# Renumbering the rows of q and k in a hybrid attention block on one Trainium2 core

## The chip, the cores and the metric

The kernel runs on one core of a Trainium2 chip. The metric is device microseconds (us) of one execution; the figure for the kernel before is the median of three. A core has five instruction streams that run side by side and wait for each other through semaphores: PE (TensorE matrix products), DVE (VectorE), ACT (ScalarE), POOL (GpSimd) and SP (SyncE). Here SP does no arithmetic: it issues all DMA transfers of the program, one after the other. PE works on tiles of 128 partitions and writes to PSUM; all other tiles lie in SBUF, which has 128 partitions as well.

## The reference, cut to what matters

One decoder block on 1024 tokens of 1024 features, in float32. Its token-mixing half projects the normed input into the heads of two mixers and attends in both:

```python
h = rms_norm(x, g_attn_pre[l]) * (1 + sc_a) + sh_a
proj = h @ w_in[l]
qa = partial_rope(proj[..., :o1].reshape(b, s, A_Q_HEADS, HEAD_DIM), cos, sin)
ka = partial_rope(proj[..., o1:o2].reshape(b, s, A_KV_HEADS, HEAD_DIM), cos, sin)
...
qb = partial_rope(proj[..., o3:o4].reshape(b, s, B_HEADS, HEAD_DIM), cos, sin)
kb = partial_rope(proj[..., o4:o5].reshape(b, s, B_HEADS, HEAD_DIM), cos, sin)
...
oa = banded_attention(qa.reshape(b, s, A_KV_HEADS, A_GROUP, HEAD_DIM), ka, va,
                      A_WINDOW - 1, sink=sink_a[l])
ob = dilated_mixture_attention(qb, kb, vb).reshape(b, s, B_W).astype(x.dtype)
mixed = jnp.concatenate([rms_norm(oa, g_mix_a[l]), rms_norm(ob, g_mix_b[l])], axis=-1)
x = x + gt_a * rms_norm(mixed @ w_out[l], g_attn_post[l])
h = rms_norm(x, g_mlp_pre[l]) * (1 + sc_m) + sh_m
x = x + gt_m * rms_norm(jnp.square(jax.nn.relu(h @ w_up[l])) @ w_down[l], g_mlp_post[l])
```

Mixer A has 8 query heads and 2 key heads of 64 features, mixer B has 8 of each. The rotation (`partial_rope`) touches the first 16 features of a head. A score is a sum over a head's 64 features, so the order in which these features are summed is free as long as q and k have the same one.

## The kernel before, in words

Each float32 operand of a product is split into a high part that is exact in PE's fast float32r format and the low rest. The projections take three products for one (high times high, low times high, high times low); the scores take a q whose 128 contraction rows hold each feature twice.

The work has stages. Up to about 60 us, x is loaded, normed and transposed, the modulation vectors are computed, and the first projection runs. From there to about 410 us six units are projected (units 0 and 1 are the two key heads of A with their four query heads each, units 2 to 5 are two heads of B each) in two halves x of 512 tokens and three column blocks c of 128, and the attention of the units that are ready runs between these products. Then come the output projection, and from about 570 us a squared-ReLU MLP.

A column block of the projection leaves PSUM in `evac` (L734). Block c = 0 holds the rotated features and is rotated on DVE (L757 to L760); the others are copied. In both cases the result becomes a pair of high and low part in a 4 KB-per-partition staging tile `hl`: ACT writes the high part (L763, L774), DVE or POOL the low one (L766, L777). There are five staging tiles in all (`r_stg`, L385), and they are shared with the loads of the modulation weights (`wa_st`, L994) and the gates (`gate_st`, L1034 and L1035).

From `hl` the features go by DMA to the tiles that the scores read, `qt` (128 rows x 4 x 512) and `kt` (128 rows x 2 x 1024). This is called a set-down here; it is `f_st` (L792), issued on SP at L803. Row 64 i + r of `qt` and of `kt` holds feature row r, in copy i. In a B unit both copies of q are the same, with high and low part side by side in a row, and copy 0 of k is its high part, copy 1 its low part; in an A unit q and k change places in this. So each feature is sent twice, by two DMAs. In an A unit one partition of `qt` takes the four heads of a feature from four partitions of `hl`.

Which feature stands on which partition of `hl` is set by `PARTS_A` and `PARTS_B` (L66 to L68): tuples (first partition, count, step, q or k, first row of qt or kt) for each column block. `ROWS_A` and `ROWS_B` (L70, L71) give the head feature of each row. The columns of w_in are put into that order on the host (`_columns`), and `tables` (L700) lays the cosines and sines on the partitions that hold rotated features: POOL fills `rows` (L707, L713), PE transposes it (L719), ACT copies it out (L721).

What sets the order is a planner (`Sched`, L175). Every operation is given to it with an estimated duration, what it depends on and which buffers it takes and gives back; it keeps a clock for each engine and emits the instructions in the order that these clocks give. Each engine then runs its own list strictly in that order. A DMA is planned with 0.62 us of SP for each issue and its bytes over 345 GB/s; a set-down of n issues enters as one step. A unit's scores may be planned once all set-downs of that half are planned to have landed (`st.posted`, `need`).

At most eight DMAs are under way: SP hands its DMAs to eight semaphores in turn, and an issue waits until the DMA before it on the same semaphore has landed.

Of the kernel before, what the change touches and what calls it, by code (L numbers as in the profile page):

```python
# [10 lines left out]
F32 = mybir.dt.float32  # L11
# [22 lines left out]
def _split_const(value, top, bits, count):  # L34
    parts, rest, unit = [], value, 2.0 ** (top - bits)
    for _ in range(count):
# [26 lines left out]

PARTS_B = (((0, 64, 2, "q", 0), (1, 64, 2, "k", 0)), ((0, 64, 2, "q", 32), (1, 64, 2, "k", 32)), ())  # L66
PARTS_A = (((0, 32, 2, "q", 0), (64, 32, 2, "q", 32), (1, 64, 2, "k", 0)),
           ((0, 96, 1, "q", 8), (96, 32, 1, "q", 40)), ((0, 64, 1, "q", 48),))  # L68

ROWS_B = [*range(0, 8), *range(16, 24), *range(8, 16), *range(24, 64)]  # L70
ROWS_A = [*range(0, 8), *range(16, 40), *range(8, 16), *range(40, 64)]  # L71


def _columns():

    out = []
    for u in range(6):
        if u > 1:
            q = [512 + 128 * u + 64 * h for h in range(2)]
            k, v = [x + 512 for x in q], [x + 1024 for x in q]  # L80
            parts, rows = PARTS_B, ROWS_B
        else:
            g = u
            q, k, v = [256 * g + 64 * h for h in range(4)], [512 + 64 * g], [640 + 64 * g]
            parts, rows = PARTS_A, ROWS_A
        for c in range(3):
            got = [h + d for h in v for d in range(64)] if c == 2 else []
            got = [0] * (P - len(got)) + got
            for p, n, step, whose, row in parts[c]:
                heads = q if whose == "q" else k  # L90
                got[p:p + n * step:step] = [h + rows[row + r] for r in range(n // len(heads)) for h in heads]
            out += got
    return out

# [254 lines left out]
def hybrid_block(ctx: ExitStack, tc: tile.TileContext, x, positions, w_ada, b_ada, g_attn_post, w_in, w_out,  # L349
# [34 lines left out]
    r_pj, r_x, r_t, r_s, r_o, r_d = Res(2), Res(1), Res(2), Res(2), Res(1), Res(0)  # L384
# [96 lines left out]
    r_wa, r_acc = Res(NWA), Res(2)  # L481
# [20 lines left out]
    def place0(name):  # L502
        return p0.tile([P, 1024], F32, name=name, tag="wa", bufs=NWA)
# [196 lines left out]
    def tables(groups, place, r_place, r_bank, bank, deps):  # L700

        for i in range(2):
# [20 lines left out]
                                   gives=[(r_bank, 1)], prio=2))  # L723

    e_tab = [[], []]
    tables([(0, 2, 4), (1, 2, 1)], lambda: place0("rows"), r_wa, r_t,
           lambda: pt.tile([P, 4, P], F32, name="ptab", tag="t"), [[], []])


# [4 lines left out]
    def evac(u, x, c, get_ps, done, r_bank):  # L734

        isb = u > 1
        parts = (PARTS_B if isb else PARTS_A)[c]
        cs = slice(512 * x, 512 * x + 512)
        b = {}
        e_q.setdefault((u, x), [])  # L740
        e_k.setdefault((u, x), [])

        def posted():
            n_in[u, x] = n_in.get((u, x), 0) + 1
            if n_in[u, x] == 3:
                st.posted += 1

        def f_new():
            b["f"] = stage("hl")[:].rearrange("p (s t) -> p s t", s=2)
            b["t"] = b["f"].bitcast(F32R)  # L750

        if c == 0:
            def f_rope():
                f_new()
                ps, t = get_ps(), b["f"][:, 1]
                cos, sin = tabs[0][:, cs], tabs[1]
                V.tensor_tensor(t[64:128], ps[0:64], sin[0:64, cs], ALU.mult)  # L757
                V.tensor_tensor(t[0:64], ps[64:128], sin[64:128, cs], ALU.mult)
                V.tensor_tensor(ps[:], ps[:], cos, ALU.mult)
                V.tensor_tensor(t, t, ps[:], ALU.add)  # L760
            e0 = e_rot[u, x] = op("DVE", 4 * t_dv(512), f_rope, [done] + e_tab[x], takes=[(r_stg, 1)],
                                  gives=[(r_bank, 1)], prio=2)
            eh = op("ACT", t_sb(512), lambda: A.copy(b["t"][:, 0], b["f"][:, 1]), [e0], prio=2)  # L763

            def f_lo(eng):
                return lambda: eng.tensor_tensor(b["t"][:, 1], b["f"][:, 1], b["f"][:, 0], ALU.subtract)  # L766
            el = op(("DVE", "POOL"), (t_dv(512), t_ptt(512)), (f_lo(V), f_lo(G)), [eh], prio=2)
        elif parts:
            n = P if c < 2 else parts[-1][1]
            sc_ = scl[0] if isb else None  # L770

            def f_hi():
                f_new()
                A.mul(b["t"][:n, 0], get_ps()[:n], -0.125 if sc_ is None else sc_[:n])  # L774

            def f_lo():
                V.scalar_tensor_tensor(b["t"][:n, 1], get_ps()[:n], -0.125 if sc_ is None else sc_[:n],  # L777
                                       b["f"][:n, 0], ALU.mult, ALU.subtract)
            eh = op("ACT", t_ps(512) + AP_COST, f_hi, [done, e_rot[u, x]], takes=[(r_stg, 1)], prio=2)
            el = op("DVE", t_dv(512) + AP_DV, f_lo, [eh], gives=[(r_bank, 1)] if c < 2 else [], prio=2)  # L780

        if parts:
            for whose in ("k", "q") if c == 0 else ("q", "k"):
                mine = [a for a in parts if a[3] == whose]
                if not mine:
                    continue
                both = isb == (whose == "q")
                nh = 2 if isb else 4 if whose == "q" else 1
                for s_ in ((0, 1) if not both else (None,)):
                    new = c == 0 and whose == "k" and s_ in (0, None)  # L790

                    def f_st(s_=s_, new=new, mine=mine, whose=whose, nh=nh, both=both):  # L792
                        if new:
                            if not x:
                                ks[u] = kring.tile([P, 2, 1024], F32R, name="kt", tag="kt")
                            qs[u, x] = qring.tile([P, 4, 512], F32R, name="qt", tag="qt")
                        dst = qs[u, x][:] if whose == "q" else ks[u][:, :, cs]
                        for p0_, n_, step, _, row in mine:
                            src = b["f"][p0_:p0_ + (n_ - 1) * step + 1:step]
                            m_ = n_ // nh  # L800
                            for i in range(2) if both else (s_,):
                                o = dst[64 * i + row:64 * i + row + m_].bitcast(F32)
                                nc.sync.dma_start(o, src if both else src[:, s_])  # L803
                    if new:
                        e_new[u, x] = Ev()
                    last = (whose == ("q" if c == 0 or not isb else "k")) and s_ in (1, None)

                    def after(new=new, last=last):
                        if new:
                            e_new[u, x].t = 0.0  # L810
                        if last and c < 2:
                            posted()
                    by = sum(a[1] * 2048 * (4 if both else 1) for a in mine)
                    e = load(f_st, by, [eh if s_ == 0 else el] + ([] if new else [e_new[u, x]]),
                             takes=[(r_k, 1 - x), (r_q, 1)] if new else [], prio=-12, n=len(mine) * (2 if both else 1),
                             gives=[(r_stg, 1)] if last else [], after=after)
                    (e_q if whose == "q" else e_k)[u, x].append(e)
        if c < 2:
            return
        nh = 2 if isb else 1  # L820
        o = P - 64 * nh

        def f_vt():
            b["vt"] = prp.tile([P, 512], F32, name="vt", tag="vt", bufs=1)
            A.copy(b["vt"][:64 * nh], get_ps()[o:])
        e = op("ACT", t_ps(512), f_vt, [done] + ([el] if parts else []), takes=[(r_vt, 1)], gives=[(r_bank, 1)], prio=2)

        def f_pv():
            b["pv"] = px.tile([P, 4, 64 * nh], F32, name="pv", tag="x")
            for j in range(4):  # L830
                T.transpose(b["pv"][:, j], b["vt"][:64 * nh, j * P:(j + 1) * P], ident[:64 * nh, :64 * nh])
        e = pe_op("post", 0.43, f_pv, [e], takes=[(r_x, 1), (r_v, 1)], gives=[(r_vt, 1)])

        def part(s_):
            return vs[u, x][:, :, :nh, s_], b["pv"][:].rearrange("p j (h d) -> p j h d", h=nh)

        def f_vh():
            vs[u, x] = vring.tile([P, 4, 2, 2, 64], F32R, name="v_hl", tag="v")
            A.copy(*part(0))

        def f_vl():
            V.tensor_tensor(part(1)[0], part(1)[1], part(0)[0].bitcast(F32), ALU.subtract)
        e = op("ACT", t_ps(256 * nh), f_vh, [e], prio=2)
        op("DVE", t_dv(256 * nh), f_vl, [e], gives=[(r_x, 1)], prio=2, after=posted)
# [1230 lines left out]
```

## Time and profile before

| | |
|---|---|
| median of three runs | 1163.08 us (1161.61 to 1167.61) |
| the profiled execution | 1161.99 us |
| its span, first to last instruction | 1160.2 us |
| PE busy | 1117.1 us, 96% of the span |
| DVE, ACT, POOL busy | 815.4, 639.2 and 261.1 us |
| mean granted TensorE clock | 0.986 |
| DMA | 185.31 MB, 51.1% of 16 engines' span on SP's queue |

Busy time is summed over instructions, so that 96% leaves some 43 us in which PE ran nothing. The profile's views give for any stretch of time how long each engine was busy, the granted clock of TensorE, the share of the 16 DMA engines' time that was in use and the rate in GB/s. The view of waits names, for an instruction that had to wait, what ended the wait; a wait for several semaphores is put down to one of them only, so the tile's name is to be read with care. The chain of waits follows the work that ended last back to what released it.

### The profile page before, as it was taken

To read this page: it belongs to the slowest core of one execution; us is meant where nothing else is said; L and a number is where in the kernel's file an instruction comes from. 1 tells how busy PE (TensorE), PEld (TensorE's weight loads), DVE (VectorE), ACT (ScalarE), POOL (GpSimd) and SP (SyncE) were. 2 spreads that over 40 slices of the span, in tenths; PEclk is the share of its full clock that TensorE was granted. 3 is DMA by queue.
4 is the path that set the end of the run, shared out by engine and by line. 5 is a ranking of instruction groups with operands and counts; after the bars stand their busy time and mean duration, and the time that the engine had idled before them with its cause. 6 is when DMAs were issued, how large, how long until landed. Compare 5 with 4: busy or idle time off the path is not lost.

```text
span 1160.2 us, 15646 instructions
## 1 busy us (share of the span) xinstructions
PE 1117.1 (96%) x5416; PEld 926.6 (80%) x5416; DVE 815.4 (70%) x1380; ACT 639.2 (55%) x1105; POOL 261.1 (23%) x344
## 2 busy tenths in 40 slices
PE   8989989999999899998999999999999999999996
PEld 7768778788888787887788888888888888888885
DVE  7848576566666775658969665499653796547998
ACT  7949676455555774667676524563233732246542
POOL 2347667566663441112000000000000000000002
PEclk9989989999999989999999999999999999999998
DMA  9477857465545614554683057812369212585103
GB/s 351 161 174 168 168 120 182 111 153 122 134 102 130 156 48 139 193 181 182 257 314 118 19 207 274 315 50 89 120 220 326 106 55 73 184 306 181 37 19 146
DMA packets 90944, 185.31 MB, mean 160 GB/s; under 512 B 8432, under 2 KB 31088, under 8 KB 90864
## 3 DMA queue, kind: packets, MB, share of 16 engines
q1 hardware_dynamic: 90864, 184.30, 51.1%
q8 instruction: 43, 0.70, 0.3%
q14 instruction: 37, 0.30, 0.1%
HBM read 137.08 MB, written 28.31 MB: 143 GB/s over the span
## 4 chain that ended last, share of the span: by engine, by line
PE 70%; DVE 10%; DMA 7%; issue 4%; POOL 4%; ACT 3%; SPq 2%; DVEq 0%; POOLq 0%; ACTq 0%
PE mlp_ps L1898 16%; PE mlp_ps L1899 16%; PE mlp_ps L1897 16%; PE pj L861 3%; PE pj L864 3%; PE pj L862 3%; PE s_ps L1122 2%; PE o_ps L1257 1%; DMA wa<-in_w_ada 1%; SPq L803 1%; PE pt_ps L1227 1%; DMA wa_st<-in_w_ada 1%; DVE hw L1668 1%; PE pt_ps L1230 1%; PE s_ps L1177 1%
## 5 line engine op out<-in xcount | busy, mean ns | idle before, releaser
L1897 PE MATMUL mlp_ps<-hw 128*128 128x512 f32 x896 | 349.7, 390 | 1.2 <-ACT hw L1659 1.2
L1898 PE MATMUL mlp_ps<-hw 128*128 128x512 f32 x896 | 348.7, 389 | 1.1 <-DVE hw L1665 1.1
L1899 PE MATMUL mlp_ps<-hw 128*128 128x512 f32 x896 | 348.6, 389 | 0.0
L1897 PEld LDWEIGHTS mlp_ps<-hw 128*128 128x128 f32 x896 | 168.2, 188 | 36.8 <-ACT hw L1659 1.6
L1898 PEld LDWEIGHTS mlp_ps<-hw 128*128 128x128 f32 x896 | 168.2, 188 | 36.8 <-DVE hw L1665 1.4
L1899 PEld LDWEIGHTS mlp_ps<-hw 128*128 128x128 f32 x896 | 168.2, 188 | 34.9
L1668 DVE TENSOR_TENSOR hw<-w,hw 128x1024 fp32r<-128x1024 f32 x96 | 114.5, 1219 | 94.7 <-ACT hw L1661 94.4
L1661 ACT CAST hw<-w 128x1024 fp32r<-128x1024 f32 x96 | 97.5, 1047 | 129.8 <-PE mlp_ps L1899 97.5
L1997 POOL TENSOR_TENSOR st<-st,nhalf 128x1 f32<-128x1 f32 x8 | 7.8, 978 | 601.9 <-DVE st L1995 601.9
L861 PE MATMUL pj<-hw,w_hl 128*128 128x512 f32 x240 | 104.2, 434 | 0.0
L864 PE MATMUL pj<-hw,w_hl 128*128 128x512 f32 x240 | 95.5, 398 | 0.0
L862 PE MATMUL pj<-hw,w_hl 128*128 128x512 f32 x240 | 95.3, 397 | 0.0
L1245 DVE TENSOR_TENSOR ph<-pt_ps,ph 128x512 fp32r<-128x512 f32 (+1 forms) x110 | 69.7, 648 | 36.0 <-ACT ph L1241 35.7
L1661 ACT CAST hw<-u 128x1024 fp32r<-128x1024 f32 x48 | 48.7, 1052 | 64.6 <-PE mlp_ps L1899 64.6
L1241 ACT CAST ph<-pt_ps 128x512 fp32r<-128x512 f32 (+1 forms) x110 | 59.5, 555 | 32.1 <-PE pt_ps L1230 27.0
L1668 DVE TENSOR_TENSOR hw<-u,hw 128x1024 fp32r<-128x1024 f32 x48 | 57.0, 1218 | 18.2 <-ACT hw L1661 18.2
L1148 ACT ACTIVATE p_sb<-p_sb,mn 128x128 f32<-128x128 f32 (+3 forms) x64 | 49.7, 777 | 36.3 <-DVE mn L1141 34.9
L1955 DVE TENSOR_TENSOR yacc<-yacc,mlp_ps 128x512 f32<-128x512 f32 x96 | 62.1, 681 | 3.3 <-PE mlp_ps L1899 3.3
L1153 POOL TENSOR_SCALAR p_sb<-p_sb,den 128x128 f32<-128x128 f32 (+3 forms) x64 | 49.0, 775 | 47.8 <-DVE den L1151 44.6
L1010 POOL TENSOR_TENSOR ada_acc<-ada_acc,wa_st 128x512 f32<-128x512 f32 x42 | 55.5, 1320 | 3.5
L864 PEld LDWEIGHTS pj<-hw,w_hl 128*128 128x128 f32 x240 | 45.6, 190 | 10.7
L1473 PE MATMUL y_ps<-hw,oh 128*128 128x512 f32 x128 | 51.7, 404 | 0.0
(205 smaller groups left out, 2010.6 us busy)
## 6 DMA issues: line engine op xcount, KB each, us to landing
hw<-s_dram SPq DMA_DIRECT2D x84, 512.0 KB
wa_st<-in_w_ada SPq DMA_DIRECT2D x32, 512.0 KB
w<-in_w_up SPq DMA_DIRECT2D x32, 512.0 KB
w<-in_w_down SPq DMA_DIRECT2D x32, 512.0 KB
s_dram<-hw SPq DMA_DIRECT2D x28, 512.0 KB
w_st<-in_w_in SPq DMA_DIRECT2D x36, 256.0 KB
x_sb<-in_x SPq DMA_DIRECT2D x16, 512.0 KB
wa<-in_w_ada SPq DMA_DIRECT2D x32, 256.0 KB
```

The source lines that it names most:

```text
L861: T.matmul(ps, w[:, 0, n], h[0], start=(k == 0), stop=False)
L862: T.matmul(ps, w[:, 1, n], h[0], start=False, stop=False)
L864: T.matmul(ps, w[:, 0, n], h[1], start=False, stop=(k == KC - 1))
L1010: G.tensor_tensor(ada.acc[:, :512], ada.acc[:, :512], wa[:, j], ALU.add)
L1241: A.copy(b["ph"][:, 0, :w], b["pt"][:, :w])
L1245: V.tensor_tensor(b["ph"][:, 1, :w], b["pt"][:, :w], b["ph"][:, 0, :w].bitcast(F32), ALU.subtract)
L1661: A.copy(out[j][0], flat(src[j]))
L1668: V.tensor_tensor(out[j][1], flat(src[j]), out[j][0].bitcast(F32), ALU.subtract)
L1897: T.matmul(ps[m][:], sh, mh, start=starts and k == 0, stop=False, **kw)
L1898: T.matmul(ps[m][:], sh, ml_, start=False, stop=False, **kw)
L1899: T.matmul(ps[m][:], sl, mh, start=False, stop=k == 3, **kw)
L1955: e = op("DVE", t_dv(512), lambda: V.tensor_tensor(y(), y(), ps[m][:], ALU.add), [e, ml.e_y[tb, n]], gives=gives, prio=1)
```

## The change

The rows of `qt` and `kt` are numbered anew. Row 2 r + i now holds feature row r in copy i, so that the two copies alternate, and a part of the tables gets a sixth number, the step between its feature rows. With it one DMA's rows lie spread over the tile: a B part fills every fourth partition, A's k every second, and A's q is cut into pieces of 16, 32 and 16 feature rows (one for each column block) that fill every eighth, every fourth and every eighth partition. Before, a DMA filled neighbouring partitions, and A's q was cut into 8 + 8, 24 + 8 and 16 rows. `ROWS_A` and `ROWS_B` follow, and the table of cosines for k of A has its eight features on every eighth partition of `hl` where they had stood on every second.

```diff
-PARTS_B = (((0, 64, 2, "q", 0), (1, 64, 2, "k", 0)), ((0, 64, 2, "q", 32), (1, 64, 2, "k", 32)), ())
-PARTS_A = (((0, 32, 2, "q", 0), (64, 32, 2, "q", 32), (1, 64, 2, "k", 0)),
-           ((0, 96, 1, "q", 8), (96, 32, 1, "q", 40)), ((0, 64, 1, "q", 48),))
-
-ROWS_B = [*range(0, 8), *range(16, 24), *range(8, 16), *range(24, 64)]
-ROWS_A = [*range(0, 8), *range(16, 40), *range(8, 16), *range(40, 64)]
+PARTS_B = (((0, 64, 2, "q", 0, 2), (1, 64, 2, "k", 0, 2)), ((0, 64, 2, "q", 1, 2), (1, 64, 2, "k", 1, 2)), ())
+PARTS_A = (((0, 64, 2, "q", 0, 4), (1, 64, 2, "k", 0, 1)), ((0, 128, 1, "q", 1, 2),), ((0, 64, 1, "q", 2, 4),))
+
+FIRST_B = [*range(0, 8), *range(16, 24), *range(8, 16), *range(24, 32)]
+ROWS_B = [FIRST_B[r // 2] if r % 2 == 0 else 32 + r // 2 for r in range(64)]
+ROWS_A = [r // 4 if r % 4 == 0 else 16 + 3 * (r // 4) + r % 4 - 1 for r in range(64)]
...
-            for p, n, step, whose, row in parts[c]:
+            for p, n, step, whose, row, ds in parts[c]:
                 heads = q if whose == "q" else k
-                got[p:p + n * step:step] = [h + rows[row + r] for r in range(n // len(heads)) for h in heads]
+                got[p:p + n * step:step] = [h + rows[row + ds * r] for r in range(n // len(heads)) for h in heads]
...
-    tables([(0, 2, 4), (1, 2, 1)], lambda: place0("rows"), r_wa, r_t,
+    tables([(0, 2, 4), (1, 8, 1)], lambda: place0("rows"), r_wa, r_t,
...
-                        for p0_, n_, step, _, row in mine:
+                        for p0_, n_, step, _, row, ds in mine:
                             src = b["f"][p0_:p0_ + (n_ - 1) * step + 1:step]
                             m_ = n_ // nh
                             for i in range(2) if both else (s_,):
-                                o = dst[64 * i + row:64 * i + row + m_].bitcast(F32)
+                                o = dst[2 * row + i:2 * row + i + 2 * ds * (m_ - 1) + 1:2 * ds].bitcast(F32)
                                 nc.sync.dma_start(o, src if both else src[:, s_])
```

The number of set-down DMAs falls in the A units, from twelve to eight for each half (two for k, and ten or six for q); their bytes stay. With fewer issues in a step, the planner's estimates and so the order change. The first place is the row of set-downs of unit 0, first half, on SP (`kt` and `qt` are the tiles set down, `hl` the staging tile; sizes are partitions x pieces x floats of the destination). Before:

```order
L803 DMA kt<-hl 64x2x512 x2
L803 DMA qt<-hl 8x4x512 x4
L803 DMA qt<-hl 24x4x512
L803 DMA qt<-hl 8x4x512
L803 DMA qt<-hl 24x4x512
L803 DMA qt<-hl 8x4x512
L803 DMA qt<-hl 16x4x512 x2
```

Now, with the second half behind it:

```order
L803 DMA kt<-hl 64x2x512 x2
L803 DMA qt<-hl 16x4x512 x2
L803 DMA qt<-hl 32x4x512 x2
L803 DMA qt<-hl 16x4x512 x2
L803 DMA kt<-hl 64x2x512 x2
L803 DMA qt<-hl 16x4x512 x2
L803 DMA qt<-hl 32x4x512 x2
L803 DMA qt<-hl 16x4x512 x2
```

Pairs of DMAs for the same rows have become one DMA each; nothing is moved past another transfer here.

The second place is on PE, where the first scores of the kernel (L1177) stand between the projection products of unit 1 (L861, L862, L864). One piece of the difference:

```order
-L861 MATMUL pj<-hw,w_hl 128x512
-L862 MATMUL pj<-hw,w_hl 128x512
-L864 MATMUL pj<-hw,w_hl 128x512
-L861 MATMUL pj<-hw,w_hl 128x512
-L862 MATMUL pj<-hw,w_hl 128x512
-L864 MATMUL pj<-hw,w_hl 128x512
-L861 MATMUL pj<-hw,w_hl 128x512
-L862 MATMUL pj<-hw,w_hl 128x512
-L864 MATMUL pj<-hw,w_hl 128x512
 L1177 MATMUL s_ps<-kt,qt 128x128 x8
```

Nine projection products that stood ahead of the first scores now stand behind them. Such shifts of a few products, scores and transposes follow until shortly before the first scores of unit 2; from there to the end all five engines have the same instructions in the same order as before.

The third place is on ACT, around the high part of the last column block of unit 1, second half (L774, 64 partitions), with the semaphores that each row waits for (a name that begins with DMAHW is one of the eight of the DMAs). Before:

```order
L1207 ACTIVATE p_sb<-p_sb,den_1576 128x256 [waits Activation_49] x3
L1304 COPY otmp<-o_ps 64x512 [waits PE_49]
L774 ACTIVATE hl<-pj 64x512 [waits DMAHW5_49,DMAHW7_49,DMAHW4_49,DMAHW0_49]
L539 CAST w_hl<-w_st 128x512 [waits DMAHW1_49]
L1304 COPY otmp<-o_ps 64x512 [waits DVE_49,PE_49]
L1241 CAST ph<-pt_ps 128x512 [waits PE_49]
L825 COPY vt<-pj 64x512 [waits DVE_49]
```

Now:

```order
L1207 ACTIVATE p_sb<-p_sb,den_1548 128x256 [waits Activation_49]
L774 ACTIVATE hl<-pj 64x512 [waits DMAHW7_49,DMAHW6_49,PE_49]
L1304 COPY otmp<-o_ps 64x512 [waits PE_49]
L539 CAST w_hl<-w_st 128x512 [waits DMAHW0_49]
L825 COPY vt<-pj 64x512 [waits DVE_49]
L1304 COPY otmp<-o_ps 64x512 [waits DVE_49,PE_49]
```

The staging tile that this row writes was free once four set-downs of q had landed; it now is another tile, last used by a gate's load and store. The copy `vt` (L825), which PE's transposes of v wait for, stands behind L774 in both.

## The prediction

> **What bounds the kernel now.** I read the busy time by stretches first, since only some stages can feel this change.
>
> ```profile
> 60.00:90.00 30.00, 24.48 (x112) 19.57 (x112) 13.65 (x31) 12.15 (x30) 13.59 (x18) 0.89 0.76 181
> 90.00:120.00 30.00, 29.49 (x176) 25.13 (x175) 26.19 (x83) 27.39 (x81) 24.58 (x41) 1.00 0.77 177
> 120.00:150.00 30.00, 24.98 (x137) 20.35 (x136) 17.12 (x53) 21.19 (x59) 19.89 (x39) 0.93 0.71 149
> 180.00:210.00 30.00, 27.48 (x143) 22.69 (x142) 19.13 (x48) 18.31 (x41) 21.31 (x24) 0.95 0.66 149
> 210.00:240.00 30.00, 30.00 (x168) 25.41 (x168) 18.15 (x50) 13.34 (x26) 13.90 (x16) 0.99 0.59 130
> 570.00:1160.00 590.00, 580.06 (x2556) 479.23 (x2554) 423.75 (x467) 274.37 (x376) 7.76 (x8) 0.99 0.46 162
> ```
>
> Columns: stretch, its length, busy time of PE, PE's weight loads, DVE, ACT and POOL, granted clock, DMA share, GB/s. PE is full in most stretches, the last 590 us among them, and that part sets nothing down. But three stretches between 60 and 210 us lose 5.5, 5.0 and 2.5 us of PE, and in the same three the granted clock is below 1. The waits of PE from 60 to 215 us, the three stalls one by one and the three stretches behind them:
>
> ```profile
> PE s_ps L1177 <- DMA kt<-hl: 5.5, 1, 5.5
> PE pv L831 <- ACT tab L721: 5.0, 1, 5.0
> PE pv L831 <- DVE ot L1293: 2.5, 1, 2.5
> ...
> 77.50:83.00 5.50, 0.00 (x0) 0.03 (x1) 1.55 (x3) 0.32 (x1) 0.00 (x0) 0.81 0.86 185
> 143.70:148.70 5.00, 0.00 (x0) 0.00 (x0) 3.79 (x10) 4.58 (x10) 3.42 (x4) 0.71 0.30 97
> 205.20:207.70 2.50, 0.00 (x0) 0.00 (x0) 0.42 (x1) 0.91 (x2) 1.44 (x2) 0.91 0.28 89
> 83.00:87.80 4.80, 4.80 (x17) 3.76 (x18) 3.07 (x12) 2.75 (x10) 1.80 (x4) 0.50 0.71 155
> 148.70:152.60 3.90, 3.89 (x16) 3.49 (x17) 1.72 (x8) 1.69 (x7) 3.77 (x8) 0.50 0.35 69
> 207.70:210.70 3.00, 3.00 (x11) 2.71 (x12) 1.84 (x3) 1.36 (x3) 2.92 (x4) 0.51 0.41 97
> ```
>
> Each stall is followed by 4.8, 3.9 and 3.0 us at half clock, in which half the time is lost. So the stalls cost 5.5 + 2.4 = 7.9, 5.0 + 1.95 = 6.95 and 2.5 + 1.5 = 4.0 us, together 18.9. The chain of waits, at the three places, shows what stands behind each:
>
> ```profile
> 67.47 0.73 SPq L803
> ...
> 78.45 4.46 DMA kt<-hl
> 83.00 1.94 PE s_ps L1177 x8
> ...
> 89.24 0.23 PE pj L861
> ...
> 135.32 8.68 DMA qt<-hl
> 144.02 0.33 ACT hl L774
> 148.71 0.69 PE pv L831 x4
> ...
> 201.62 5.50 DMA o_dram<-ot
> 207.23 0.43 DVE ot L1293
> 207.70 1.12 PE pv L831 x4
> ```
>
> Stall 1: the first scores need the set-downs of unit 0, first half, which SP issues from 67.47 us on. The tile in the row is the second half's `kt`, issued last; the scores need only the first half's, which land just before it. Stall 2: a set-down of q takes 8.68 us from issue to landing, ACT stands at L774 for its staging tile, and PE's transposes of v need the ACT row behind it. Stall 3: the small store of an attention result takes 5.5 us, since it queues behind set-downs of B; DVE waits for its tile, and PE for DVE. All three are set-downs that move too slowly. How slowly, against a plain load, is in the DMA view of three stretches (0.8 us of weight loads; 2 us of B's q; 4 us of A's pieces):
>
> ```profile
> DMA packets 174, 0.33 MB, mean 407 GB/s; under 512 B 15, under 2 KB 15, under 8 KB 174
> q1 hardware_dynamic: 174, 0.33, 105.4%
> ...
> DMA packets 82, 0.27 MB, mean 135 GB/s; under 512 B 16, under 2 KB 16, under 8 KB 82
> q1 hardware_dynamic: 82, 0.27, 102.5%
> ...
> DMA packets 321, 0.56 MB, mean 140 GB/s; under 512 B 47, under 2 KB 47, under 8 KB 321
> q1 hardware_dynamic: 321, 0.56, 63.5%
> ```
>
> B's q goes to 32 neighbouring partitions and keeps all 16 engines busy, yet moves a third of what a load to 128 partitions does. A's pieces, most of them 8 rows, leave a third of the engines' time unused and move no more.
>
> **The change part by part.** One half of an A unit, from the page's sizes and counts over four such halves:
>
> ```profile
> kt<-hl SPq DMA_DIRECT2D x8, 256.0 KB
> qt<-hl SPq DMA_DIRECT2D x24, 64.0 KB
> qt<-hl SPq DMA_DIRECT2D x8, 192.0 KB
> qt<-hl SPq DMA_DIRECT2D x8, 128.0 KB
> 69.31 8.35 SPq L803 DMA_DIRECT2D qt<-hl  x10
> ```
>
> 2 x 256 + 6 x 64 + 2 x 192 + 2 x 128 = 1536 KB, 1.57 MB, before and after. Issues fall from 12 to 8, sixteen over the four halves; at 0.84 us each (8.35 over 10, waits included) that is 3.3 us of SP per half, of worth only where SP is what ends the wait.
>
> What rate the spread rows reach, no row shows. The ends are 135 GB/s (32 neighbouring rows; nothing gained) and 407 (rows on all 128 partitions, as now, but from HBM). The spread set-down resembles the first in its source and the second in its destination, so I take the middle by ratio, 234 GB/s, and keep both ends.
>
> The Trainium skill (SBUF — State Buffer, Door 1: The DMA port swizzle) says that a transfer's rate follows the number of 16 ports its partitions reach, and that 32 or 64 neighbouring ones reach eight; its figures are 189 GB/s for partitions 0 to 31 and 328 for all. The trace has 135 in place of the 189, and the measured row decides. The same section speaks against part of this change: by its formula, rows on every eighth partition reach eight ports only, so A's 16-row pieces would stay slow. At 135 for those 512 KB and 234 for the rest, a half takes 8.4 us, not 6.7, and the forecast would be 1.7 us later; no run here shows it.
>
> *Stall 1.* The loads ahead drain between 68 and 72 us:
>
> ```profile
> 68.00:70.00 2.00, 2.00 (x11) 1.65 (x10) 1.48 (x3) 1.63 (x3) 1.90 (x2) 1.00 1.06 309
> 70.00:72.00 2.00, 2.00 (x12) 1.41 (x11) 0.42 (x1) 0.47 (x2) 2.00 (x3) 1.00 1.02 154
> ```
>
> I take 70.5. Then 1.57 MB at 234 take 6.7 us, to 77.2, some 77.4 with the semaphore. PE arrives nine products of 0.23 us sooner, at 77.5 - 2.1 = 75.4: 2.0 us of stall, and behind it one stretch at half clock as after stall 3, 1.5 us. The nine products come later and lose nothing. Gain 7.9 - 3.5 = 4.4. Ends: at 407 SP's issues are the limit and no stall is left, 7.9; at 135 the rows land at 70.5 + 11.6 = 82.1, the stall is 6.7 and the half clock as now: a loss of 1.2.
>
> *Stall 2.* The wait is gone in its form: ACT's L774 no longer waits for four set-downs, but for a gate's load and store, and those queue behind the same traffic, faster now. Left: nothing (6.95 gained) to all of it (0). I take a gain of 5.0, near the upper end, because 8.68 us of queue held the wait and the set-downs in it are now quicker and fewer.
>
> *Stall 3.* The order here is unchanged. Ahead of the store lie four q set-downs of 256 KB; at 135 each takes 1.94 us, at 234 1.12. The last two alone bring the store 1.6 us forward, all four 3.3. I take 0.8 us of stall left and no half clock: gain 3.2, ends 0 and 4.0.
>
> *The order between 75 and 175 us.* PE has scores and transposes earlier, in front of products that could fill a wait. In 90 to 120 us ACT is busy 27.39 of 30 us, so a pull forward can run into it. Nothing shows the price; 0 to 8 us (one more stall like the second), and I take 1.5.
>
> *The table of A's k.* Its copies have another step; they run before 53 us, and POOL idles 8.04 us before its next work:
>
> ```profile
> L713 POOL COPY rows<-cosw x18: 296/308/866, 43.0 to 133.7; 128x64 f32<-128x64 f32 x18
> 61.67 1.29 POOL L544 TENSOR_TENSOR w_hl<-w_st,w_hl 128x512 fp32r<-128x512 f32 x1 [8.04 <-ACT w_hl L539]
> ```
>
> Four copies, none slower than 0.87 us against 0.31: at most 2.2 us in that gap, 0.
>
> *B's set-downs elsewhere.* They run beside products that fill PE (30.00 of 30 us from 210 to 240): 0. Where that cover is missing, stall 3 shows the cost, 4.0.
>
> Sum: 4.4 + 5.0 + 3.2 - 1.5 = 11.1 us. The profiled execution took 1161.99 us, 1.8 more than its span and 1.1 less than the median, so 1150.9 there; I say 1151.
>
> **The rivals.**
>
> Slower. The rate does not rise, because moving from SBUF to SBUF is the limit and not the rows. For it: B's q has all engines busy at 102.5% and still moves 135. Against: that 135 and the pieces' 140 at 63.5% are not one rate per busy engine (132 and 220). Then stall 1 costs 1.2 more, stalls 2 and 3 stay, and the reordering costs 2 to 8: 1165 to 1171. It decides below some 150 GB/s, where stall 1 gains nothing.
>
> The stalls move. The set-downs are faster, but the earlier scores run into ACT or POOL, and half of the 12.6 us comes back: 1156 to 1161. For it is the ACT row of 90 to 120 us; against, that ACT is busy 12.15 and 21.19 us of 30 in the stretches that hold stalls 1 and 2, and takes the pull there.
>
> All is gained. At 407 GB/s and with no new waits: 1162 - 18.9 = 1143.
>
> Hidden anyway. Fewer issues and quicker rows, but the three waits end with other transfers (loads and the gates): 1160 to 1165.
>
> **How the numbers follow.** My forecast, 1147 to 1156, has 0.50; the moved stalls 0.20; all gained 0.14; hidden 0.07; slower 0.09. From 1143 to 1163 holds all but the slower case and the edges. 0.5% of the median is 5.8 us, about what can be told from no change: faster means below 1157.3. That is the forecast, all gained and half of the moved stalls, 0.74; same is the other half and hidden, 0.17; slower 0.09.
>
> **What would show it.** Right: no wait of PE over 3 us between 60 and 215 us, the granted clock 0.95 or more in each 30 us there, the q of B above 200 GB/s, the store before 207 us landing in under 4 us; and 570 us to the end as long as now. Wrong: B's q still near 135, or a wait of PE for ACT, DVE or POOL over 2 us that the waits before do not have. The forecast fails most easily in the reordering, which is priced by nothing measured.

## The result, and the profile after

The changed kernel takes 1152.38 us in the median (1150.98 to 1155.83, five runs), the kernel before 1163.08 (1161.32 to 1167.61). The ratio is 0.9903, with a 95% interval of 0.9877 to 0.9929. The profiled execution took 1152.38 us, of which the span is 1150.4. The forecast was 1151, in a range of 1143 to 1163. The total came out almost as worked out; the profile shows that its terms did not all do so.

The busy times by stretches after the change (columns as before: length; PE, weight loads, DVE, ACT, POOL; granted clock, DMA share, GB/s), and the waits of PE from 60 to 215 us:

```profile
60.00:90.00 30.00, 29.07 (x159) 24.07 (x158) 20.10 (x59) 19.08 (x55) 18.55 (x25) 1.00 0.80 257
90.00:120.00 30.00, 28.50 (x158) 22.54 (x155) 22.33 (x63) 24.10 (x65) 20.87 (x35) 1.00 0.51 144
120.00:150.00 30.00, 24.19 (x135) 20.56 (x136) 16.81 (x56) 20.64 (x64) 23.02 (x45) 0.94 0.40 125
180.00:210.00 30.00, 30.00 (x168) 25.41 (x167) 20.06 (x56) 17.23 (x40) 23.42 (x25) 1.00 0.49 159
```

```profile
PE s_ps L1177 <- DMA o_dram<-ot: 5.0, 1, 5.0
PE s_ps L1177 <- DVE mn L1192: 1.2, 1, 1.2
PE s_ps L1177 <- DMA kt<-hl: 0.9, 1, 0.9
PE s_ps L1177 <- DMA qt<-hl: 0.7, 1, 0.7
```

The first stall is gone but for 0.9 us, and the third wholly: PE is busy 29.07 of the 30 us from 60 and all 30 from 180, at full clock. But from 120 to 150 us PE is idle for 5.8 us (5.0 before), and it is another wait: 5.0 us of scores (L1177) where PE had stood at the transposes of v (L831). The chain of waits at the first scores and at this place:

```profile
73.07 3.12 DMA kt<-hl
76.19 1.08 PE s_ps L1177 x8
```

```profile
136.91 1.29 POOL ada_acc L1010
138.20 0.68 POOL wa_st L1009
138.96 1.30 POOL ada_acc L1010
...
140.40 0.27 SPq L994
...
140.76 0.56 SPq L803
...
143.38 1.96 DMA o_dram<-ot
145.35 1.19 PE s_ps L1177 x4
```

The first scores now start at 76.19 us, not 83.00. At the second place the wait's row names a store (`o_dram`), but what the scores need is q: the second copy of its last piece in unit 1, second half, which SP issued at 140.76 us. It landed at 144.90, and PE's waits for the scores passed one after the other from 144.92 on; the store landed only at 145.62, when the scores had begun. DVE had finished that copy's data at 134.37:

```profile
133.69 0.68 DVE L777 SCALAR_TENSOR_TENSOR hl<-pj,hl 64x512 fp32r<-64x512 f32 x1 [0.19 <-ACT hl L774]
```

SP could not send it, because the load of modulation weights (L994) stands ahead of it, and that load waited for POOL to be done with its staging tile (L1010, to 140.26). So the set-down stood ready for 6.4 us behind an instruction that had nothing to do with it.

The rate of the set-downs, in the 5.6 us in which the first half of unit 0 lands (70.4 to 76 us), and in 1.7 us with two set-downs of B's q (217.6 to 219.3 us), which had moved 135 GB/s before:

```profile
DMA packets 902, 1.59 MB, mean 284 GB/s; under 512 B 129, under 2 KB 129, under 8 KB 901
q1 hardware_dynamic: 901, 1.58, 97.8%
...
DMA packets 189, 0.54 MB, mean 321 GB/s; under 512 B 32, under 2 KB 64, under 8 KB 189
```

### The profile page after: what moved, and what is told of

Read it like the earlier page. It is cut to its first block, busy times and chain, and to the rows that moved or that the text cites. A ratio compares the mean times of both kernels' runs of the same rounds, so it can differ in the third digit from the quotient of the medians.

```text
span 1150.4 us, 15603 instructions
## 1 busy us (share of the span) xinstructions
PE 1113.0 (97%) x5416; PEld 921.2 (80%) x5416; DVE 818.7 (71%) x1381; ACT 638.8 (56%) x1108; POOL 259.5 (23%) x340
## 4 chain that ended last, share of the span: by engine, by line
PE 74%; DVE 10%; ACT 5%; DMA 4%; issue 4%; POOL 2%; SPq 1%; DVEq 0%; POOLq 0%; ACTq 0%
PE mlp_ps L1898 16%; PE mlp_ps L1899 16%; PE mlp_ps L1897 16%; PE pj L861 4%; PE pj L864 3%; PE pj L862 3%; PE s_ps L1122 3%; PE o_ps L1257 2%; DMA w_st<-in_w_in 1%; PE pt_ps L1227 1%; PE pt_ps L1230 1%; PE y_ps L1475 1%; DVE hw L1668 1%; PE o_ps L1262 1%; PE y_ps L1473 1%
## 5 line engine op out<-in xcount | busy, mean ns | idle before, releaser
L861 PE MATMUL pj<-hw,w_hl 128*128 128x512 f32 x240 | 102.4, 427 | 0.0
L864 PE MATMUL pj<-hw,w_hl 128*128 128x512 f32 x240 | 94.6, 394 | 0.0
L862 PE MATMUL pj<-hw,w_hl 128*128 128x512 f32 x240 | 94.5, 394 | 0.0
L1010 POOL TENSOR_TENSOR ada_acc<-ada_acc,wa_st 128x512 f32<-128x512 f32 x42 | 54.6, 1299 | 3.5
L864 PEld LDWEIGHTS pj<-hw,w_hl 128*128 128x128 f32 x240 | 45.1, 188 | 10.4
```

The lines of the kernel that those rows point to most:

```text
L861: T.matmul(ps, w[:, 0, n], h[0], start=(k == 0), stop=False)
L862: T.matmul(ps, w[:, 1, n], h[0], start=False, stop=False)
L864: T.matmul(ps, w[:, 0, n], h[1], start=False, stop=(k == KC - 1))
```

## The experiments

A table over all of them first: when PE started its n-th product, counted in each kernel's own order, against the kernel before (us, from the two traces of each pair; negative is sooner). Products up to 340 are common to all; the first scores come next, stall 2 lies between 680 and 780, stall 3 between 980 and 1010, and 5415 is the last product.

```
                              400    560    680    780    980   1010   2200   5415
changed kernel               -6.9   -7.4   -5.1   -4.9   -5.8   -9.7  -10.2   -9.3
new rows, order of before    -7.2   -8.2   -7.6  -12.9  -13.6  -17.6  -16.8  -16.7
old rows, new order          +4.1  +10.2  +11.2  +12.3  +13.2  +14.8  +16.8  +16.6
changed, one pair exchanged  -6.9   -7.2   -4.9  -10.4  -11.6  -15.6  -11.6   -9.8
new rows, old cuts           -5.7   -5.2   -5.0  -10.2  -10.8  -14.8  -13.8  -13.5
A only                       -6.8   -7.7   -7.1  -12.5  -11.3  -13.7   -8.4   -6.0
B only                       -0.1   -0.2   -0.1   -0.1   -0.2   -4.1   -3.5   -3.3
alternating copies only      -4.6   -4.5   -4.4   -8.2   -7.6   -9.3   -5.6   -5.7
changed, copies apart        -2.0   -1.8   -0.3   +1.2   +2.8   +0.2   +0.2   +2.2
```

**How fast is a set-down, by itself?** The sums above rest on a rate for which the trace had no row. A kernel that does nothing but DMAs sends eight of one form, waits for them (in `gate`, DVE reads the eight tiles and writes `src`), and goes on to the next form. Of a form, `m` is the number of rows, `ds` their step, `n` and `w` the pieces of a row and their floats, `ss` the step of the source's rows.

```diff
+    for m, ds, first, n, w, ss in SETS:
+        for k in range(8):
+            o = dst[k][first:first + ds * (m - 1) + 1:ds]
+            rows = m * n if n > 1 else m
+            s = src[0:(rows - 1) * ss + 1:ss]
+            if n == 4 or n == 2:
+                nc.sync.dma_start(o[:, 0:n * w].rearrange("p (a t) -> p a t", a=n), s[:, 0:w])
+            else:
+                nc.sync.dma_start(o[:, 0:w], s[:, 0:w])
+        gate()
```

> This kernel leaves the whole computation out. It sends eight DMAs of one form at a time, and then the next form, once DVE has seen the first eight land: rows of 2 KB or 4 KB from a staging tile to 8, 16, 24, 32, 64 or 128 rows of another tile, neighbouring or on every second, fourth or eighth partition; last, eight loads from HBM to 128 rows. Its time says nothing; the rate of each form does. Theory (the rows are the limit): 32 neighbouring rows about 135 GB/s as in the kernel before; 32 rows on every fourth partition 230 to 330; from SBUF to all 128 rows near the 400 of a load. Rival (moving from SBUF to SBUF is the limit): all forms of 256 KB between 130 and 180, the one with 128 rows too. The Trainium skill (SBUF - State Buffer, Door 1: The DMA port swizzle) counts ports: 32 rows on every second partition reach eight, as 32 neighbouring ones, so no gain there, and on every fourth partition sixteen; 16 rows reach four as neighbours and eight on every second, fourth or eighth partition alike. By that rule the form of 16 rows gains the same from any step, and 32 rows gain only from the step of four.

Measured, from the first packet of a form to the end of its last:

```
rows of the destination        KB per DMA    GB/s    median packet
32 neighbouring                256           133     516 ns (4 KB)
32, every second               256           136     504 ns (4 KB)
32, every fourth               256           393     159 ns (4 KB)
32 neighbouring                256           133     278 ns (2 KB)
32, every fourth               256           372      86 ns (2 KB)
64 neighbouring                256           137     497 ns (4 KB)
64, every second               256           393     161 ns (4 KB)
24 neighbouring                192           160     166 ns (2 KB)
16 neighbouring                128           118     305 ns (2 KB)
16, every 2nd / 4th / 8th      128           189 / 202 / 200   84 ns (2 KB)
8 neighbouring                 64            62      305 ns (2 KB)
128 (all)                      256           373     86 ns (2 KB)
```

The DMA view of steady stretches of the forms with 32 neighbouring rows, and with 32 rows on every fourth partition:

```profile
DMA packets 469, 1.53 MB, mean 127 GB/s; under 512 B 96, under 2 KB 96, under 8 KB 469
q1 hardware_dynamic: 469, 1.53, 103.7%
```

```profile
DMA packets 491, 1.62 MB, mean 405 GB/s; under 512 B 96, under 2 KB 96, under 8 KB 491
q1 hardware_dynamic: 491, 1.62, 100.4%
```

Both keep all engines busy; one moves three times what the other does, and more than the 230 to 330 expected. So the rival "SBUF to SBUF is the limit" falls: the eight loads from HBM at the end of this kernel moved 313 GB/s, less than the spread rows did. And alternating the copies is not enough for q of B: every second of 64 neighbours stays at 136.

**Rows and order apart.** The change moves two things: rows (with pieces), and, through the planner's count of issues, the order. Each was made alone. New rows with the order of before:

```diff
-                    takes=[(r_k, 1 - x), (r_q, 1)] if new else [], prio=-12, n=len(mine) * (2 if both else 1),
+                    takes=[(r_k, 1 - x), (r_q, 1)] if new else [], prio=-12, n=len(mine) * (2 if both else 1) + (not isb and whose == "q" and c < 2),
```

> The changed rows and pieces, but the planner is told the issues of before for q of A, so that the order of all engines is that of before (with the merged DMAs). Theory (the gain comes from quicker set-downs, the order costs about 2 us and brings the wait behind the modulation load): PE comes to the first scores at 77.5 us, after the rows have landed (76.1): no stall there; the wait of ACT for q's set-downs near 144 us shrinks from 5.0 us to under 1.5; the third stall is gone: 1161.99 - 18.9 + 1.5 = 1144.6, that is 1143 to 1148. Rival (the new order is part of the gain): 1152 or more.

Measured: 1144.97 us, ratio to before 0.9832 (0.9811 to 0.9853). It beats both kernels. No wait of PE from 60 to 215 us is over 0.5 us:

```profile
PE o_ps L1269 <- DVE ph L1245: 0.5, 2, 0.3
PE o_ps L1269 <- ACT ph L1241: 0.5, 1, 0.5
```

Old rows and pieces with the new order, in the kernel before:

```diff
-                             takes=[(r_k, 1 - x), (r_q, 1)] if new else [], prio=-12, n=len(mine) * (2 if both else 1),
+                             takes=[(r_k, 1 - x), (r_q, 1)] if new else [], prio=-12, n=2 if both else 1,
```

> Rows, pieces and DMAs of before, but the planner is told the issues of the changed kernel, so that the order is that of the changed kernel (with the pieces in two). Theory (the order gains nothing): PE comes to the first scores some 2 us sooner and waits for rows that still land at 82.5: a stall of 7 us; the set-down of q behind the modulation load makes the second stall, about 5; the third stays: 1163 to 1168, slower than before or the same. Rival (the new order brings the gain): 1152 to 1156.

Measured: 1178.8 us, ratio 1.0113 (1.0083 to 1.0143), slower than either theory had it.

```profile
PE s_ps L1177 <- DMA kt<-hl: 8.9, 1, 8.9
PE s_ps L1177 <- DMA o_dram<-ot: 5.6, 1, 5.6
PE pt_ps L1234 <- POOL p_sb L1209: 2.9, 2, 1.5
```

The second row is the new stall of the changed kernel: it belongs to the order, not to the rows. The third is part of a loss that neither theory had: 6.1 us between products 400 and 560 (+4.1 to +10.2 in the table), where PE waits for POOL and the granted clock is 0.93 from 90 to 120 us; no run takes it apart. The four kernels give the sum of the change: the rows alone are worth 1.7%, the order alone costs 1.1% with the old rows and, from 0.9832 to 0.9903, 0.7% with the new ones (1144.97 against 1152.38, 7.4 us, in two series whose kernels before differ by 1.1 us).

**Is the load on SP the whole cause of the new stall?** In the changed kernel the two neighbours on SP were exchanged:

```diff
-        el = load(f_load, 524288, takes=[(r_stg, 1)], prio=20)
+        el = load(f_load if i != 6 else lambda: held.append(f_load), 524288, takes=[(r_stg, 1)], prio=20)
...
                                 nc.sync.dma_start(o, src if both else src[:, s_])
+                        while held:
+                            held.pop()()
```

> The changed kernel, with one pair of neighbours on SP exchanged: the second copy of the last piece of q of unit 1, second half, is issued ahead of the modulation load that had held it up from 134.4 to 140.8 us. Theory (that load is the whole cause of the new stall at 140 us): the rows land near 136.7, PE does not wait at 140, and the half clock behind it goes too: 1152.4 - 5.0 - 1.7 = 1145.7, 1145 to 1148. Rival (the scores that follow would wait for ACT or POOL all the same): 1150 to 1153.

Measured: 1151.32 us (1149.8 to 1155.52), as the rival had it in time, but not for its reason. The wait at 140 us is gone, and PE is 5 to 6 us ahead of the changed kernel from there on (-10.4 against -4.9 in the table, -15.6 against -9.7 later). It then loses most of this near 400 us (-11.6 against -10.2 at product 2200). Three stretches of this kernel, the last two of which overlap:

```profile
140.00:145.30 5.30, 5.30 (x37) 4.73 (x36) 3.46 (x17) 4.13 (x15) 3.40 (x9) 1.00 0.63 163
390.00:400.90 10.90, 5.60 (x24) 4.11 (x23) 5.79 (x19) 5.20 (x11) 7.18 (x6) 0.68 0.35 108
394.00:404.20 10.20, 6.99 (x22) 4.90 (x21) 4.69 (x14) 5.30 (x9) 4.17 (x5) 0.50 0.38 116
```

and its chain of waits there (lines stand two higher in this kernel):

```profile
392.43 2.40 POOL hw L1359
...
394.85 0.33 SPq L1374
...
395.28 4.48 DMA o_sb<-o_dram
...
399.79 1.05 ACT oh L1433
...
400.88 0.80 PE y_ps L1475
```

It is the same pattern again: the load of a gate (L1374) stands ahead of the load of the attention's result (`o_sb`) on SP. In the changed kernel's instructions this load waits for a reader on ACT (L1348 there); with the pair exchanged, the staging tiles are handed out in another turn, and it waits for POOL's product at L1359. PE waits 2.6 us for it, up to 400.88. The 10.2 us at half clock begin at 394.0, before this wait, so the wait did not start them, and the kernel before has 6.83 us of half clock at the same products, where the changed kernel's profile happens to have none. So a part of what is lost here need not be an effect of the exchange. The cause of the stall at 140 us is shown; that its removal is worth the whole 6.7 us is not, since the edit made another wait.

**What in the rows does it?** The kernels of the next four experiments keep the order of before on PE, DVE, ACT and POOL, so that they compare with the 0.9832 above. First, new rows with A's q cut in 8 + 8, 24 + 8 and 16 rows as before, on top of the version with the order of before:

```diff
-                            for i in range(2) if both else (s_,):
-                                o = dst[2 * row + i:2 * row + i + 2 * ds * (m_ - 1) + 1:2 * ds].bitcast(F32)
-                                nc.sync.dma_start(o, src if both else src[:, s_])
+                            cut = (8, 24)[c] if not isb and whose == "q" and c < 2 else m_
+                            for r0, r1 in ((0, cut), (cut, m_)):
+                                for i in (range(2) if both else (s_,)) if r1 > r0 else ():
+                                    at = 2 * (row + ds * r0) + i
+                                    o = dst[at:at + 2 * ds * (r1 - r0 - 1) + 1:2 * ds].bitcast(F32)
+                                    from_ = b["f"][p0_ + nh * step * r0:p0_ + (nh * r1 - 1) * step + 1:step]
+                                    nc.sync.dma_start(o, from_ if both else from_[:, s_])
```

> Rows spread as in the changed kernel, order of before, but A's q is still sent in pieces of 8 + 8, 24 + 8 and 16 rows, twelve DMAs for a half as before. Theory (the rows bring the gain, the pieces little): the last rows of the first half land some 3 us later than with eight DMAs (four more issues of 0.65 us on SP), near 78 to 79 us, about when PE comes at 77.5: 1145 to 1149. Rival (fewer and larger pieces bring much of it): 1152 to 1158.

Measured: 1148.89 us, ratio 0.9844 (0.981 to 0.9878). The larger pieces are worth a little at most: the interval overlaps that of the version with them. In the trace it is 3.2 us behind that version at the end (-13.5 against -16.7): a wait of 1.6 us at the first scores, and as much again by product 560.

Only B's rows spread, and only A's rows and pieces changed. In both, a part with a step of 0 lies as before; the first has such parts, and `ROWS_A` and the table of before, for A, the second such parts and `ROWS_B` of before for B (and the order of before):

```diff
-                                o = dst[2 * row + i:2 * row + i + 2 * ds * (m_ - 1) + 1:2 * ds].bitcast(F32)
+                                at, by_ = (2 * row + i, 2 * ds) if ds else (64 * i + row, 1)
+                                o = dst[at:at + by_ * (m_ - 1) + 1:by_].bitcast(F32)
```

> Only B's rows are spread; A's rows and pieces, and the order of all engines, are those of before. Theory: stall 3 goes with its half clock, 4.0 us, and nothing else: 1158 to 1161. Rival (B's slow set-downs also feed the other stalls or later places): under 1155. Rival (stall 3 needs A as well): 1162 to 1165.

> The counterpart: A's rows and pieces as in the changed kernel, B's as before, order of all engines that of before. Theory: stalls 1 and 2 go (14.9 us of the profiled execution), stall 3 stays: 1148 to 1151, so that the gains of the two halves of the change add up to the 19 us of both. Rival (stall 3 moves or grows, as PE comes to it sooner): 1152 to 1156.

Measured: B only 1160.51 us, ratio 0.9953 (0.9934 to 0.9973); A only 1149.53, ratio 0.9861 (0.9818 to 0.9904). Their gains, 0.5% and 1.4%, add up to the 1.7% of both within the intervals. With B only, the first two stalls stand as before and the third is gone (lines stand up to two higher here):

```profile
PE s_ps L1179 <- DMA kt<-hl: 5.3, 1, 5.3
PE pv L833 <- ACT tab L722: 4.7, 1, 4.7
PE o_ps L1271 <- DVE ph L1247: 1.0, 1, 1.0
```

With A only, the largest wait left there is stall 3, now 1.5 us, so that it neither stayed nor grew, as the two sides had it, but shrank. That profiled execution (1155.83 us, the slowest of its runs) gave back 7.7 us after 210 us, in pieces that no single wait of its trace accounts for; the largest is a wait of 1.9 us for POOL near 246 us with 3.4 us of half clock behind it.

Last, how far the rows must be spread. The kernel before, with nothing changed but the place of the copies:

```diff
-                                o = dst[64 * i + row:64 * i + row + m_].bitcast(F32)
+                                o = dst[2 * row + i:2 * (row + m_) + i - 1:2].bitcast(F32)
```

> The kernel before, order and pieces included; only the rows' places change: copy i of feature row r stands in row 2 r + i instead of 64 i + r, all else equal. So k of A fills every second partition of all 128, q of B every second of 64 neighbours, A's pieces of 8, 24 and 16 rows every second of 16, 48 and 32. By the rates measured alone (64 rows on every second partition 393 GB/s, 32 rows on every second 136, 16 rows on every second at least 189): theory (reach counts): k of A becomes quick and the pieces somewhat, q of B not at all. Stalls 1 and 2 shrink by half or more, stall 3 stays: 1152 to 1158. Rival (the alternating copies alone bring the gain of the rows): 1145 to 1148. Rival (only the full spread helps): 1161 to 1165.

Measured: 1154.57 us, ratio 0.9893 (0.9856 to 0.9929). The three stalls, the third one first:

```profile
PE pv L831 <- DVE ot L1293: 2.2, 1, 2.2
PE s_ps L1177 <- DMA qt<-hl: 1.8, 1, 1.8
PE pv L831 <- ACT tab L721: 1.7, 1, 1.7
```

And the changed kernel (its order too), with the copies 64 rows apart, each spread over one half:

```diff
-                                o = dst[2 * row + i:2 * row + i + 2 * ds * (m_ - 1) + 1:2 * ds].bitcast(F32)
+                                o = dst[64 * i + row:64 * i + row + ds * (m_ - 1) + 1:ds].bitcast(F32)
```

> The changed kernel, its pieces, issues and order, but the copies stand 64 rows apart again: copy i of row r in 64 i + r. Each set-down is as spread as before within one half of the tile, and reaches 64 partitions at most. Theory (reach over all 128 brings the gain): k of A (64 neighbours, 137 GB/s alone) and q's 32-row pieces and B (every second of 64, 136 GB/s) are slow again; one half of an A unit takes 3.8 + 2.6 + 3.9 = 10.3 us and not 5.8, so the first scores wait some 5 us and a half clock follows, and the third stall comes back with its 4 us: 1160 to 1168. Rival (larger and fewer pieces bring the gain): 1151 to 1154.

Measured: 1164.25 us, ratio 0.9993 (0.9969 to 1.0017): pieces, issues and order of the changed kernel, and no gain over the kernel before. Its waits:

```profile
PE s_ps L1177 <- DMA o_dram<-ot: 4.9, 1, 4.9
PE s_ps L1177 <- DMA kt<-hl: 3.0, 1, 3.0
PE s_ps L1177 <- DVE mn L1192: 1.3, 1, 1.3
PE pv L831 <- DVE ot L1293: 1.3, 1, 1.3
```

The fair partner of this kernel is not the kernel before but the one with old rows and the new order (1.0113), as it has that order too. Against that one it gains 1.2%, and its first wait is 3.0 us instead of 8.9: fewer and larger pieces, spread over one half, do help, and no run parts the two under this order. Reaching both halves of the 128 partitions brings the other 0.9% (0.9993 to 0.9903), and without it the change gains nothing over the kernel before. One line, the alternating copies, brings some two thirds of what the rows bring (1.07% of 1.68%); by the rates measured alone that is A's k (64 rows on every second partition), and A's pieces may add to it, while q of B needs the step of four. Where B's rows have it, PE gains 3.9 to 4.0 us at stall 3 (between products 980 and 1010 of the table); where they have not, as here, with the alternating copies alone and with A only, 1.7 to 2.6 us.

**Why are 16 spread rows quick?** In the first series they kept packets of 84 ns for 2 KB, where 32 neighbouring rows took 278; but less was asked of them. The same kernel, with other forms:

> Again rates alone, the whole computation left out. In the first series 16 rows on every second, fourth or eighth partition kept packets of 84 ns at about 200 GB/s, though they reach no more ports than 32 neighbouring rows, which had fallen to 133; but these DMAs of 128 KB were issued every 0.64 us, so that no more than 205 GB/s was asked for, while the forms of 256 KB asked for 410. Here 32 and 64 neighbouring rows get 128 KB each, and 16 spread rows 256 KB. Theory (what is asked of eight ports decides: they hold about 200 and fall to 135 when asked for 400): the first two forms about 200, the 16-row forms of 256 KB about 135. Rival (the place of the rows decides, whatever is asked): the first two forms 135, the 16-row forms over 350.

```
rows of the destination        KB per DMA    GB/s    median packet
32 neighbouring                128           164     213 ns (2 KB)
64 neighbouring                128           179     172 ns (2 KB)
16, every 2nd / 4th / 8th      256           212 / 206 / 205   318 to 329 ns (4 KB)
```

Neither had it. Sixteen spread rows hold about 200 GB/s whatever is asked (189 to 212), so 128 KB at each issue (205 GB/s) just fits. Thirty-two or 64 neighbours move 164 to 179 when asked for 205, and only 133 to 137 when asked for twice that. Where the difference comes from is open.

## Why the prediction was right, and where it was not

The time was right (1151 against 1152.38) and so was the main cause: set-downs that moved too slowly because of where their rows lie. The terms were not all right, and that their sum came so near is in part luck: stall 2 gave 5.2 us less than its term, while stall 1 (2.5 us), stall 3 (0.7) and the rest (0.5) gave 3.7 more.

```
step                     forecast gain    measured gain (trace)
stall 1                       4.4         6.9   (product 400)
order, 75 to 140 us          -1.5        -1.8   (-6.9 to -5.1)
stall 2                       5.0        -0.2   (-5.1 to -4.9)
stall 3                       3.2         3.9   (-5.8 to -9.7)
between and after             0           0.5   (+0.9 before stall 3, -0.4 after it)
sum                          11.1         9.3
```

*Stall 1.* The mechanism was right, the rate too low: 234 GB/s had been taken, and forms with 32 or 64 spread rows reach 372 to 393 alone. In the kernel the half landed in 5.8 us instead of the 6.7 (70.3 to 76.1), close to SP's eight issues (67.32 to 72.98, one every 0.65 us or so), and no half clock followed.

*Stall 2.* This step failed: "the wait is gone in its form" held, and nearly all of the gain was then taken by a wait that the sum did not have. The step looked at what ACT now waits for; the second copy of the same piece, which in the new order stands behind a modulation load on SP, was overlooked. With the order of before, this stall is indeed worth 5.3 us (-7.6 to -12.9 in the table).

*Stall 3.* Right; all of it went. The store of the attention's result, 5.50 us before, lands 1.9 us after its issue:

```profile
o_dram<-ot SPq DMA_DIRECT2D x1, 64.0 KB, 1.9
```

*The order.* 1.5 us had been taken from a range of 0 to 8, "one more stall like the second". It was just that: the direct part is 1.8 us, and with the new stall the order costs 7.4 us (1152.38 against 1144.97). The value at the upper end was the right one. Seen this way, the term of stall 2 was right in size (5.3 against 5.0) and it is the order that was put 5.9 us too low; stall 1 made up for 2.5 us of that.

*The rivals.* That SBUF to SBUF is the limit is refuted. That the stalls move was partly true, on SP rather than on ACT or POOL as it had been put. "All is gained", 1143, is what the rows do by themselves: 1144.97 with the order of before. "Hidden anyway" is refuted for stalls 1 and 3, which are gone; at stall 2 a load did take the wait over, in the new order only.

*The signs named beforehand.* Two failed in the same place: a wait of PE of 5.0 us where none over 3 was allowed, and a clock of 0.94 from 120 to 150 us instead of 0.95. The others held: the rate of B's q (321 GB/s), the store (1.9 us), and the last part, which is as long as before (product 2840 to the last one takes 584.6 us in both).

*The rule on ports.* The Trainium skill (SBUF — State Buffer, Door 1: The DMA port swizzle) counts the ports that a transfer's partitions reach, and the rates of forms of 256 KB fall into its groups: eight ports at 133 to 212 GB/s, sixteen at 372 to 393, where the Trainium skill has 189 and 328. That the 16-row pieces reach eight ports only fits their 205 to 212, but the count alone does not tell 133 from 212; and it cost nothing here, since 128 KB per issue ask for no more. The 1.7 us that the rule would have added did not come.

## What to carry to other kernels

Spread the rows of an SBUF-to-SBUF DMA over both halves of the partitions: 32 or 64 rows moved 133 to 137 GB/s as neighbours and 393 on every fourth or second partition, with the same bytes and issues. When a change alters a planner's input, run it once with the old order; here the order took back 7 of the 17 to 19 us that the rows brought. And look on each in-order queue, the one that issues DMAs above all, for an instruction that waits for an unrelated buffer ahead of one that PE needs.

## What the hardware did that was not expected

The first of eight DMAs to 32 neighbouring rows is not slow: in the first eighth of its form's packets the median is 167 ns for 4 KB, and in the later eighths it is 521 to 527 ns. The slow rate shows only once further DMAs are under way; whether it is their number or the length of the burst, no run here parts.

Under full demand 16 spread rows hold 205 to 212 GB/s, and 32 neighbouring rows only 133, less than the 164 that they move when half as much is asked. No experiment here explains it.

The record of the granted clock shows half clock in stretches of 3.41, 6.83 and 10.24 us, multiples of one step, after PE has been idle for part of the time. The same products near 400 us had 6.83 us of it in the kernel before and in the version with the order of before, and none in the changed kernel's profile. By these rows a step of 3.41 us at half clock costs PE up to 1.7 us, so it is an estimate that two runs of one kernel can differ by some us for this alone; the changed kernel's five spread over 4.9 us, with mean clocks of 0.991 to 0.995.
